# Low parts one piece behind the high parts in the paired products, and transposes two turns later

## The chip, the cores and the metric

The kernel runs on one core of one Trainium2 chip. A core has TensorE (PE, matrix products into PSUM; its weight loads are listed as PEld), VectorE (DVE), ScalarE (ACT), GpSimd (POOL) and SyncE (SP), which issues the transfers. Each engine works through its own queue of instructions in order, and waits for others by semaphores. The metric is the device time of one execution in microseconds, the median of the runs.

## The reference, cut to what matters

The reference is a two-block network on 256 tokens of width 2048, all in float32. The change touches only the last part of the second block, its feed-forward layer (`D_FF` is 5632):

```python
h2 = _rmsnorm(x, ffn_norm_w[l])
g, u = jnp.split(jnp.einsum('bsd,df->bsf', h2, w_gate_up[l]), 2, axis=-1)
x = x + jnp.einsum('bsf,fd->bsd', jax.nn.silu(g) * u, w_down[l])
return _rmsnorm(x, final_norm_w)
```

## The kernel before

All products are made in near-float32 accuracy from a number format with fewer bits. Each operand is split into a high part (ScalarE copies it into the shorter format) and a low part (VectorE subtracts the high part from the original). A product is then three matmuls: high by high, low by high, high by low. The activations are split once. The weights stream from HBM in pieces of 256 x 512 numbers (512 KB), and each piece is split as it arrives: `hl` (line 382) puts ScalarE's copy (line 385, tile `wh`) and VectorE's subtraction (line 386, tile `wl`) into the queues one behind the other.

A plain product (`Job`, `Chunk`) has 512 columns of weights; a chunk is one piece, and its twelve matmuls (lines 139 to 142) are two tiles of 128 tokens, two slices of 128 rows, three matmuls each.

The feed-forward layer has eleven blocks of 512 columns, j = 0 to 10, each with a gate and an up product. Block 0 is made of plain products. Blocks 1 to 10 are paired products (`Pair`): the first half of the inner dimension is worked as four quads, in which the four half-products of gate and up are had from seven instead of eight (P1 to P7) with sums of weights in place of one of them; the second half is plain chunks. A quad has four parts (`QuadPart`):

- g: a raw gate piece, for P1 and P2 (6 matmuls, lines 255 to 257);
- u: half of a raw up piece, for P3 (3 matmuls);
- t: two sums of raw pieces made on VectorE (`formt`, line 318), the second independent of the first, for P5 and P7 (6 matmuls);
- v: two more sums (`formv`), the second reading the first, for P6 and P4 (6 matmuls).

The list of pieces of a pair is g, u, t, v, and a gate chunk c (`PairChunk`, lines 201 to 204), four times over, and then four up chunks. At the end of the fourth quad ScalarE copies P1, P5, P7 and P6 out of PSUM (tile `ps`), and GpSimd adds them up in four operations. After the fourth gate chunk `ga_evac` makes the gate (two VectorE sums into `sg`, two SiLUs on ScalarE). After the last up chunk `ub_evac` finishes the block on VectorE (tiles `up` and `sg`).

The block is then transposed for the down product. `finish` in `ffn` (line 1830) adds a small routine, `later`, that goes on by turns: at a turn TensorE transposes half of the block (four transposes into PSUM, line 363, tile `sp`), at the next turn ScalarE and VectorE split the result (tiles `ah` and `al`), and the same again for the other half. A turn comes after each u, v and chunk (`p.side`), not after g or t.

The order of everything is written out by `drive` (line 494): before the matmuls of piece i are put into TensorE's queue, `feed` has put the splits of the pieces up to i + 4 into ScalarE's and VectorE's queues, and their loads into SyncE's. What an evacuation or a turn of `later` adds comes behind those. `la` is the distance, 3 at first and 4 from block 1 on, when `wide` (line 1894) is called. At most `nraw` raw pieces (5 from then on) are loaded and not yet dropped.

All large tiles come from 43 buffers (`Slots`), given out in the order in which they were given back. Who gets a buffer waits for the last reader of its old content. A raw piece is given back when its low part is queued, g and u when v has been formed; high and low parts when the piece's matmuls are queued; t and v in the split of v.

After blocks 0 to 3, 4 to 7 and 8 to 10 there are down products (`fd`) over what is ready: four column blocks of eight chunks in the first two thirds, five in the last. In the first of the four, a chunk waits by `needs` until the block that it reads has been transposed: block 3, 7 or 10 is needed at the seventh, seventh and fifth chunk; if its `later` has turns left then, they are taken at once (`force`).

Of the kernel before, what the change touches and what calls it, by code (L numbers as in the profile page):

```python
# [9 lines left out]
F32 = mybir.dt.float32  # L10
F32R = mybir.dt.float32r
# [5 lines left out]
P = 128  # L17
# [10 lines left out]
RAW = 4  # L28
LA = 3
# [85 lines left out]
class Chunk(Piece):  # L115
# [4 lines left out]
        self.job, self.ks, self.n = job, ks, job.n  # L120
        self.w = job.w[ks[0] * P:(ks[-1] + 1) * P, job.n0:job.n0 + job.n].rearrange("(k p) n -> p k n", p=P)

    def split(self, b):
        self.wh, self.wl = b.hl(self.raw, len(self.ks), self.n)
        b.drop(self.raw)

    def prod(self, b, outs=None, tiles=range(2)):
# [90 lines left out]
class QuadPart(Piece):  # L218
# [2 lines left out]
    def __init__(self, pair, q, raws, names, first, last):  # L221
        self.pair, self.q, self.raws, self.names, self.first, self.last = pair, q, raws, names, first, last

    def split(self, b):
        g, u = self.raws.get("g"), self.raws.get("u")
        if self.w is not None:
            self.raws[self.kind] = self.raw
        if self.kind == "g":
            self.wh, self.wl = b.hl(self.raw, 2, 512)
        elif self.kind == "u":  # L230
            self.wh, self.wl = b.hl(self.raw[:, 1:2], 1, 512)
        elif self.kind == "t":
            t = self.raws["t"] = b.slots.get([P, 2, 512], F32, "formt")
            b.tt(t[:, 0], u[:, 0], g[:, 0], ALU.subtract, b.teng[0])
            b.tt(t[:, 1], u[:, 1], u[:, 0], ALU.subtract, b.teng[1])
            self.wh, self.wl = b.hl(t, 2, 512)
        else:
            t, v = self.raws["t"], b.slots.get([P, 2, 512], F32, "formv")
            b.tt(v[:, 0], u[:, 1], t[:, 0], ALU.subtract, b.teng[2])
            b.tt(v[:, 1], g[:, 1], v[:, 0], ALU.subtract, b.teng[3])  # L240
            self.wh, self.wl = b.hl(v, 2, 512)
            b.drop(g)
            b.drop(u)
            b.slots.put(t, v)

    def prod(self, b):
        P_, q = self.pair.p, self.q
# [42 lines left out]
class Builder:  # L290
# [88 lines left out]
        for t in ts:  # L379
            self.abanks.append(self.bof.pop(id(t))[1])  # L380

    def hl(self, src, nk, n):

        wh, wl = self.slots.get([P, nk, n], F32R, "wh"), self.slots.get([P, nk, n], F32R, "wl")
        self.nc.scalar.activation(wh, src, AF.Copy)  # L385
        self.nc.vector.tensor_tensor(wl, src, wh.bitcast(F32), op=ALU.subtract)  # L386
        return wh, wl

    def drop(self, raw):
        self.slots.put(raw)  # L390
# [82 lines left out]
    def split_first(self, k):  # L473

        p = self.all[0]
        if k == 0:
            p.wh, p.wl = self.slots.get([P, KG, 512], F32R, "wh"), self.slots.get([P, KG, 512], F32R, "wl")
        self.act(p.wh[:, k], p.raw[:, k])
        self.tt(p.wl[:, k], p.raw[:, k], p.wh[:, k].bitcast(F32), ALU.subtract)
        if k == KG - 1:  # L480
            self.drop(p.raw)
            self.ns = 1

    def feed(self, n):

        while True:
            while self.nd < len(self.loads) and self.live < self.nraw:
                self.load()
            if self.ns >= min(n, len(self.all)):
                break  # L490
            self.all[self.ns].split(self)
            self.ns += 1

    def drive(self):
        self.all = [p for j in self.jobs for p in j.pieces()]
        self.loads = [p for p in self.all if p.w is not None]
        self.nd = self.ns = self.live = 0
        self.nraw, self.la = RAW, LA
        self.feed(0)
        self.begin()  # L500
        for i, p in enumerate(self.all):
            if p.begin:
                p.begin()
            self.feed(i + 1 + min(self.la, 1 + i // RAMP))
            if type(p) is Chunk and p.job.evac is None:
                break
            for ev in p.needs:
                self.force(ev)
            p.prod(self)
            p.done(self)  # L510
            if p.side:
                self.side()

        for t in range(2):
            for c, p in enumerate(self.all[i:]):
                o = self.acc()
                p.prod(self, {t: o}, [t])
                self.last_evac(t, c, o)
                self.free(o)
            self.finish(t)  # L520
# [1289 lines left out]
    def ffn(self):  # L1810
# [19 lines left out]
        def finish(j, s):  # L1830
            h, l = sl.get([P, 4, 256], F32R, f"ah{j}"), sl.get([P, 4, 256], F32R, f"al{j}")
            aT[j] = (h, l)

            def later():
                for b in range(2):
                    yield 1
                    p = self.ps()
                    for jj in range(2):
                        for t in range(2):
                            self.tr(p[:, jj * 256 + t * P:jj * 256 + (t + 1) * P], s[:, t, (2 * b + jj) * P:(2 * b + jj + 1) * P])  # L1840
                    yield 1
                    fl = lambda a: a[:, 2 * b:2 * b + 2, :].rearrange("p a b -> p (a b)")
                    self.split(fl(h), fl(l), p)
                sl.put(s)
                self.done(f"aT{j}")
            self.add(later(), urgent=True)
            if j == 10:
                for v in h3 + list(self.sx.values()):
                    sl.put(*v)
# [44 lines left out]
        def wide():  # L1894

            self.abanks = deque(list(range(4, 7)) + list(self.abanks))
            self.sbanks = deque([7])
            self.nraw, self.la = 5, 4

        ak = lambda k: (aT[k // 4][0][:, k % 4, :], aT[k // 4][1][:, k % 4, :])  # L1900
        xs = lambda q, i: [v[:, i, q % 2, :] for v in self.sx[q // 2]]
# [91 lines left out]
```

## Time and profile before

| what | value |
|---|---|
| median of 3 runs | 2350.32 us (2348.36 to 2350.64) |
| profiled execution, its own time | 2351.64 us |
| its span, first to last instruction | 2349.4 us |
| mean granted TensorE clock | 0.984 |
| busy: TensorE / VectorE / ScalarE / GpSimd | 96% / 66% / 49% / 17% |
| HBM over the span | 175 GB/s |
| ten paired products (three stretches together) | 530.5 us |
| first two down products | 89.0 and 89.5 us |

Rows of the profile give, for a group, its line, engine and operation, the tile written and those read, the number of instructions, and their time; in views by time the first number is the start in microseconds and the second the stretch that the merged instructions take, with the idle time before it and what ended it in brackets. A granted clock below 1 means that TensorE ran slower, as it does behind a pause. Matmuls overlap in the pipeline, so that a row of 0.39 us comes every 0.23 us, and a TensorE that is shown as busy may still have lost time.

### The profile page before, as it was taken

The page shows a single profiled execution, that of the slowest core. Times are in us where ns is not written, and L with a number is a line of the kernel's source. Part 1 is how long each engine was busy: PE and PEld are TensorE (multiplying, and loading weights), DVE is VectorE, ACT ScalarE, POOL GpSimd, SP SyncE. Part 2 cuts the span into 40 slices and gives each one's busy share as a digit, 9 for nine tenths or more (in the row PEclk, how much of TensorE's full clock was granted, in tenths as well). Part 3 has the DMA queues.
Part 4 walks back from the last instruction along what each step waited for, and adds up shares of the span by engine and source line. Part 5 has one row for each costly group of instructions (what it writes and reads, how often), then busy time and mean ns, then how long its engine had stood idle before and what let it go on. Part 6 is the DMA issues. An engine that isn't in the chain of part 4 may idle for free.

```text
span 2349.4 us, 27772 instructions
## 1 busy us (share of the span) xinstructions
PE 2254.9 (96%) x10396; PEld 1863.1 (79%) x10396; DVE 1541.1 (66%) x1774; ACT 1145.1 (49%) x1532; POOL 399.2 (17%) x284
## 2 busy tenths in 40 slices
PE   9999999999999999999999999998899888998898
PEld 7888888888888888888888888876678666786676
DVE  5775776456566554556867865657765777747774
ACT  6634545546545443445555544534453444534453
POOL 2020104004232010002733521101110111101111
PEclk9999999999999999999999999999999999999899
DMA  9655555464565566665455565645465444655472
GB/s 313 189 176 185 157 174 172 152 199 151 161 197 179 181 185 202 202 199 183 147 163 161 161 187 183 198 141 161 144 205 181 145 153 150 206 161 180 144 247 75
DMA packets 215046, 413.99 MB, mean 176 GB/s; under 512 B 13538, under 2 KB 20432, under 8 KB 214912
## 3 DMA queue, kind: packets, MB, share of 16 engines
q1 hardware_dynamic: 211968, 405.99, 54.5%
q0 software_dynamic: 2224, 5.13, 0.7%
q8 instruction: 81, 1.33, 0.2%
q10 hardware_dynamic: 720, 1.11, 0.1%
q14 instruction: 53, 0.43, 0.1%
HBM read 408.51 MB, written 3.67 MB: 175 GB/s over the span
## 4 chain that ended last, share of the span: by engine, by line
PE 66%; DVE 10%; ACT 5%; issue 4%; POOL 1%; ACTq 0%; DVEq 0%; POOLq 0%
PE acc L139 19%; PE acc L140 19%; PE acc L142 19%; DVE wl L386 5%; ACT wh L385 4%; PE sp L343 3%; DVE formv L318 2%; PE sp L363 2%; DVE formt L318 2%; POOL ps L318 1%; PE acc L201 1%; PE acc L202 1%; ACT ps L314 1%; PE acc L204 1%; DVE up L318 0%
## 5 line engine op out<-in xcount | busy, mean ns | idle before, releaser
L386 DVE TENSOR_TENSOR wl<-raw,wh 128x1024 fp32r<-128x1024 f32 (+2 forms) x763 | 956.5, 1292 | 318.2 <-ACT wh L385 274.6
L385 ACT ACTIVATE wh<-raw 128x1024 fp32r<-128x1024 f32 (+2 forms) x763 | 743.7, 1025 | 154.7 <-DVE wl L386 93.1
L139 PE MATMUL acc<-wh,xh 128*128 128x512 f32 (+2 forms) x864 | 339.8, 393 | 0.0
L140 PE MATMUL acc<-wh,xl 128*128 128x512 f32 (+2 forms) x864 | 336.2, 389 | 0.0
L142 PE MATMUL acc<-wl,xh 128*128 128x512 f32 (+2 forms) x864 | 230.5, 389 | 0.0
L139 PE MATMUL acc<-wh,h2h 128*128 128x512 f32 x512 | 202.2, 395 | 0.0
L140 PE MATMUL acc<-wh,h2l 128*128 128x512 f32 x512 | 199.4, 389 | 0.0
L142 PEld LDWEIGHTS acc<-wl,xh 128*128 128x128 f32 x864 | 162.8, 188 | 32.9
L140 PEld LDWEIGHTS acc<-wh,xl 128*128 128x128 f32 x864 | 162.7, 188 | 31.0
L139 PEld LDWEIGHTS acc<-wh,xh 128*128 128x128 f32 x864 | 162.7, 188 | 30.7
L318 POOL TENSOR_TENSOR ps<-ps 128x512 f32<-128x512 f32 x40 | 66.0, 1649 | 670.9 <-ACT ps L314 668.6
L139 PE MATMUL acc<-wh,ah 128*128 128x512 f32 x352 | 137.5, 391 | 0.0
L140 PE MATMUL acc<-wh,al 128*128 128x512 f32 x352 | 137.0, 389 | 0.0
L142 PE MATMUL acc<-wl,h2h 128*128 128x512 f32 x512 | 136.9, 389 | 0.0
L201 PE MATMUL acc<-wh,h3h 128*128 128x512 f32 x320 | 127.2, 397 | 0.0
L202 PE MATMUL acc<-wh,h3l 128*128 128x512 f32 x320 | 126.7, 396 | 0.0
L142 PEld LDWEIGHTS acc<-wl,h2h 128*128 128x128 f32 x512 | 96.1, 188 | 20.0
L385 ACT ACTIVATE wh<-formt 128x1024 fp32r<-128x1024 f32 x40 | 42.4, 1060 | 141.8 <-DVE formt L318 141.8
L140 PEld LDWEIGHTS acc<-wh,h2l 128*128 128x128 f32 x512 | 96.2, 188 | 18.9
L139 PEld LDWEIGHTS acc<-wh,h2h 128*128 128x128 f32 x512 | 96.2, 188 | 19.0
L385 ACT ACTIVATE wh<-formv 128x1024 fp32r<-128x1024 f32 x40 | 42.3, 1058 | 118.2 <-DVE formv L318 112.2
L142 PE MATMUL acc<-wl,ah 128*128 128x512 f32 x352 | 94.8, 389 | 0.0
(492 smaller groups left out, 3844.2 us busy)
## 6 DMA issues: line engine op xcount, KB each, us to landing
raw<-in_w_in_dram SPq DMA_DIRECT2D x328, 512.0 KB, 3.7
raw<-in_w_gate_up_dram SPq DMA_DIRECT2D x176, 512.0 KB, 4.1
raw<-in_w_down_dram SPq DMA_DIRECT2D x88, 512.0 KB, 4.0
raw<-in_w_out_dram SPq DMA_DIRECT2D x64, 512.0 KB, 3.8
raw<-in_w_branch_dram SPq DMA_DIRECT2D x48, 512.0 KB, 3.9
raw<-in_w_mem_kv_dram SPq DMA_DIRECT2D x31, 512.0 KB, 6.8
raw<-in_w_in_dram SPq DMA_DIRECT2D x8, 464.0 KB, 3.4
raw<-in_w_in_dram SPq DMA_DIRECT2D x8, 448.0 KB, 3.4
```

Source lines behind the costliest of these rows:

```text
L139: b.nc.tensor.matmul(outs[t], x, self.wh[:, kk], start=self.first and kk == 0, stop=False)
L140: b.nc.tensor.matmul(outs[t], y, self.wh[:, kk], start=False, stop=False)
L142: b.nc.tensor.matmul(outs[t], x, self.wl[:, kk], start=False, stop=self.last and kk == len(self.ks) - 1)
L201: b.nc.tensor.matmul(outs[t], x, self.wh[:, kk], start=self.first and kk == 0 and t == 1, stop=False)
L202: b.nc.tensor.matmul(outs[t], y, self.wh[:, kk], start=False, stop=False)
L204: b.nc.tensor.matmul(outs[t], x, self.wl[:, kk], start=False, stop=self.last and kk == len(self.ks) - 1)
L314: self.nc.scalar.activation(out, in_, func, **k)
L318: (self.nc.vector if eng == "v" else self.nc.gpsimd).tensor_tensor(out, a, b, op=op)
L343: self.nc.tensor.matmul(out, lhsT, rhs, start=start, stop=stop)
L363: self.nc.tensor.transpose(out, in_, self.ident if k == P else self.ident[:k, :k])
L385: self.nc.scalar.activation(wh, src, AF.Copy)
L386: self.nc.vector.tensor_tensor(wl, src, wh.bitcast(F32), op=ALU.subtract)
```

## The change

In the paired products and all that follows them, a piece's split is taken apart. `hi` puts the sums (for t and v) and ScalarE's high part into the queues; `lo` puts VectorE's low part there. `feed` lets `hi` run `ahead` pieces in front of `lo`: 0 until `wide`, 1 from then on. So the low part of a piece follows the sums and the high part of the next piece. The pieces whose low parts are queued before the matmuls of piece i are the same as before. g's and u's raw pieces are given back in `hi` of v, which now stands ahead of t's low part; t and v are given back each with its own low part.

In `later` the first half's transposes wait three turns instead of one; the second half's follow as before, so that all of it is two turns later. A down product's first turns are affected too: for block 10 two turns remain when the fifth chunk needs it.

```diff
@@ class Chunk
-    def split(self, b):
-        self.wh, self.wl = b.hl(self.raw, len(self.ks), self.n)
+    def hi(self, b):
+        self.src = self.raw
+        self.wh = b.hi(self.src)
+
+    def lo(self, b):
+        self.wl = b.lo(self.src, self.wh)
         b.drop(self.raw)
@@ class QuadPart
-    def split(self, b):
+    def hi(self, b):
         g, u = self.raws.get("g"), self.raws.get("u")
         if self.w is not None:
             self.raws[self.kind] = self.raw
         if self.kind == "g":
-            self.wh, self.wl = b.hl(self.raw, 2, 512)
+            self.src = self.raw
         elif self.kind == "u":
-            self.wh, self.wl = b.hl(self.raw[:, 1:2], 1, 512)
+            self.src = self.raw[:, 1:2]
         elif self.kind == "t":
-            t = self.raws["t"] = b.slots.get([P, 2, 512], F32, "formt")
+            t = self.src = self.raws["t"] = b.slots.get([P, 2, 512], F32, "formt")
             b.tt(t[:, 0], u[:, 0], g[:, 0], ALU.subtract, b.teng[0])
             b.tt(t[:, 1], u[:, 1], u[:, 0], ALU.subtract, b.teng[1])
-            self.wh, self.wl = b.hl(t, 2, 512)
         else:
             t, v = self.raws["t"], b.slots.get([P, 2, 512], F32, "formv")
+            self.src = v
             b.tt(v[:, 0], u[:, 1], t[:, 0], ALU.subtract, b.teng[2])
             b.tt(v[:, 1], g[:, 1], v[:, 0], ALU.subtract, b.teng[3])
-            self.wh, self.wl = b.hl(v, 2, 512)
             b.drop(g)
             b.drop(u)
-            b.slots.put(t, v)
+        self.wh = b.hi(self.src)
+
+    def lo(self, b):
+        self.wl = b.lo(self.src, self.wh)
+        if self.kind in "tv":
+            b.slots.put(self.src)
@@ class Builder
-    def hl(self, src, nk, n):
-
-        wh, wl = self.slots.get([P, nk, n], F32R, "wh"), self.slots.get([P, nk, n], F32R, "wl")
+    def hi(self, src):
+
+        wh = self.slots.get(src.shape, F32R, "wh")
         self.nc.scalar.activation(wh, src, AF.Copy)
+        return wh
+
+    def lo(self, src, wh):
+        wl = self.slots.get(src.shape, F32R, "wl")
         self.nc.vector.tensor_tensor(wl, src, wh.bitcast(F32), op=ALU.subtract)
-        return wh, wl
+        return wl
...
     def feed(self, n):
 
+        n = min(n, len(self.all))
         while True:
             while self.nd < len(self.loads) and self.live < self.nraw:
                 self.load()
-            if self.ns >= min(n, len(self.all)):
+            if self.ns >= n:
                 break
-            self.all[self.ns].split(self)
+            while self.nh < min(self.ns + 1 + self.ahead, len(self.all)):
+                self.all[self.nh].hi(self)
+                self.nh += 1
+            self.all[self.ns].lo(self)
             self.ns += 1
...
@@ ffn, finish, later
                 for b in range(2):
-                    yield 1
+                    yield 1 if b else 3
                     p = self.ps()
...
@@ ffn, wide
-            self.nraw, self.la = 5, 4
+            self.nraw, self.la, self.ahead = 5, 4, 1
```

More of the change, by code (lines that the diff above doesn't have):

```diff
@@ L481, in split_first @@
             self.drop(p.raw)
-            self.ns = 1
+            self.ns = self.nh = 1
     def feed(self, n):
+        n = min(n, len(self.all))
         while True:
@@ L496, in drive @@
         self.loads = [p for p in self.all if p.w is not None]
-        self.nd = self.ns = self.live = 0
-        self.nraw, self.la = RAW, LA
+        self.nd = self.nh = self.ns = self.live = 0
+        self.nraw, self.la, self.ahead = RAW, LA, 0
         self.feed(0)
```

## The prediction

> **What bounds the kernel now.** I read the stages of the run first (busy time of each engine in chosen stretches), then the waits inside one of them, then VectorE's and TensorE's instructions in order of time. The change touches only the feed-forward part, which begins near 1500 us. The first three rows below are the ten paired products (1 to 3, 4 to 7, 8 to 10), the last two the down products between them. (A pair ends 10.1 us after GpSimd's sums in it begin, 1614.28 - 1604.14 in rows below; I laid the bounds by that.)
>
> ```profile
> core 0: us, PE busy (x) PEld busy (x) DVE busy (x) ACT busy (x) POOL busy (x), PEclk, DMA share, GB/s
> 1562.50:1724.24 161.74, 137.24 (x565) 106.47 (x564) 124.86 (x141) 80.88 (x98) 19.78 (x12) 0.94 0.49 160
> 1813.20:2025.07 211.87, 181.06 (x740) 140.61 (x739) 163.36 (x184) 103.37 (x125) 26.39 (x16) 0.94 0.50 166
> 2114.60:2271.46 156.86, 136.81 (x552) 106.41 (x551) 121.01 (x136) 77.08 (x93) 20.87 (x14) 0.93 0.53 174
> 1724.24:1813.20 88.96, 87.99 (x392) 72.62 (x392) 49.40 (x50) 35.33 (x36) 0.00 (x0) 1.00 0.55 173
> 2025.07:2114.60 89.53, 89.53 (x400) 73.91 (x399) 49.47 (x50) 35.43 (x36) 0.00 (x0) 1.00 0.54 171
> ```
>
> In the down products TensorE is busy 99 to 100% of the time at full clock: nothing on VectorE can speed them up. In the paired products, 530.5 us together, no engine is busy all the time and the granted clock is 0.94. The rhythm shows in GpSimd's four sums, once per pair:
>
> ```profile
> 1604.14 6.83 POOL L318 TENSOR_TENSOR ps<-ps 128x512 f32<-128x512 f32 x4 [72.85 <-ACT ps L314]
> 1659.08 6.83 POOL L318 TENSOR_TENSOR ps<-ps 128x512 f32<-128x512 f32 x4 [48.12 <-ACT ps L314]
> 1714.10 6.83 POOL L318 TENSOR_TENSOR ps<-ps 128x512 f32<-128x512 f32 x4 [48.19 <-ACT ps L314]
> ```
>
> A pair takes 55.0 us (1714.10 - 1659.08). VectorE's instructions show why; this is the last quad of a pair, the rest of that pair, and the start of the next:
>
> ```profile
> 1589.28 2.96 DVE L386 TENSOR_TENSOR wl<-raw,wh 128x1024 fp32r<-128x1024 f32 x3
> 1592.15 1.28 DVE L318 TENSOR_TENSOR formt<-raw 128x512 f32<-128x512 f32 x2
> 1594.62 1.23 DVE L386 TENSOR_TENSOR wl<-formt,wh 128x1024 fp32r<-128x1024 f32 x1 [1.19 <-ACT wh L385]
> 1595.77 0.68 DVE L318 TENSOR_TENSOR formv<-raw,formt 128x512 f32<-128x512 f32 x1
> 1596.48 0.69 DVE L318 TENSOR_TENSOR formv<-raw,formv 128x512 f32<-128x512 f32 x1
> 1598.36 1.23 DVE L386 TENSOR_TENSOR wl<-formv,wh 128x1024 fp32r<-128x1024 f32 x1 [1.18 <-ACT wh L385]
> 1599.50 3.60 DVE L386 TENSOR_TENSOR wl<-raw,wh 128x1024 fp32r<-128x1024 f32 x3
> 1603.60 1.23 DVE L386 TENSOR_TENSOR wl<-raw,wh 128x1024 fp32r<-128x1024 f32 x1 [0.50 <-ACT wh L385]
> 1605.04 2.02 DVE L386 TENSOR_TENSOR wl<-raw,wh 128x1024 fp32r<-128x1024 f32 x1 [0.21 <-ACT wh L385]
> 1606.99 0.68 DVE L318 TENSOR_TENSOR sg<-acc,ps 128x512 f32<-128x512 f32 x1
> 1608.25 0.69 DVE L318 TENSOR_TENSOR sg<-acc,ps 128x512 f32<-128x512 f32 x1 [0.58 <-POOL ps L318]
> 1610.68 1.97 DVE L386 TENSOR_TENSOR wl<-raw,wh 128x1024 fp32r<-128x1024 f32 x2 [1.74 <-ACT wh L385]
> ...
> 1619.92 0.68 DVE L318 TENSOR_TENSOR up<-acc,ps 128x512 f32<-128x512 f32 x1
> ...
> 1622.69 2.96 DVE L386 TENSOR_TENSOR wl<-raw,wh 128x1024 fp32r<-128x1024 f32 x3
> ```
>
> VectorE is never waiting for TensorE here. It forms a sum, waits 1.19 us until ScalarE has rounded it, subtracts, forms the next sum, waits 1.18 us again. From 1589.28 to 1599.50 one quad takes it 10.22 us: low parts of c, g and u 2.87; sum t until its low part starts 2.47; that low part 1.15; sum v until its low part 2.59; that low part 1.14. A 1024-wide low part thus has a pitch of 1.14 and a 512-wide one 0.59. TensorE follows behind:
>
> ```profile
> 1598.38 0.50 PE L255 MATMUL acc<-wh,sh 128*128 128x512 f32 x1 [1.28 <-ACT wh L385]
> ...
> 1600.67 0.40 PE L201 MATMUL acc<-wh,h3h 128*128 128x512 f32 x1
> ...
> 1603.40 0.39 PE L201 MATMUL acc<-wh,h3h 128*128 128x512 f32 x1
> ...
> 1614.28 0.39 PE L255 MATMUL acc<-wh,h3h 128*128 128x512 f32 x1
> ```
>
> ```profile
> 1621.54 0.45 PE L363 MATMUL sp<-ident,sg 128*128 128x128 f32 x1 [5.05 <-DVE sg L327]
> ...
> 1630.04 0.60 PE L363 MATMUL sp<-ident,sg 128*128 128x128 f32 x4
> 1630.39 0.48 PE L255 MATMUL acc<-wh,h3h 128*128 128x512 f32 x1
> ```
>
> The twelve matmuls of a chunk take 2.73 us (1600.67 to 1603.40), 0.2275 each. So the 33 of a quad with its chunk need 7.5 us, and a pair (180, and two groups of four transposes at 0.35) 41.65. TensorE could run a pair in 41.65, VectorE is busy 41 us per pair ((124.86 + 163.36 + 121.01) / 10), and the difference is waiting: for ScalarE in every quad, and once per pair TensorE's transposes, which stand behind the next pair's first two pieces and wait 5.05 us for sg.
>
> **The change part by part.** *Low parts one piece later.* VectorE's order in a quad becomes: low c, low g, both sums of t, low u, both sums of v, low t, low v. Nothing is added to any engine. Two independent 512-wide operations follow at 0.60:
>
> ```profile
> 1629.18 0.68 DVE L318 TENSOR_TENSOR al<-sp,ah 128x512 fp32r<-128x512 f32 x1
> 1629.78 0.68 DVE L318 TENSOR_TENSOR formv<-raw,formt 128x512 f32<-128x512 f32 x1
> ```
>
> So t's sums occupy 1.20, v's dependent sums 0.71 + 0.60 = 1.31 (1596.48 - 1595.77, then a pitch). t's high part is ready 2.47 after its sums start; u's low part (0.60) and v's sums fill 3.11, no wait is left. v's is ready 2.59 after its sums start, and 1.31 + 1.14 = 2.45 are filled: 0.14 of waiting. The quad: 2.28 + 1.20 + 0.60 + 1.31 + 1.14 + 0.14 + 1.14 = 7.81 instead of 10.22. Saved 2.41, four times a pair: 9.64. What hides ScalarE's rounding now is u's low part and v's sums; without that cover each of the two costs its 1.2 again.
>
> The other waits of that VectorE view also go, because the high part is already queued on ScalarE before the copies of P1, P5, P7, P6 and the two SiLUs: 0.50, 0.21, 1.74, and 0.58 since sg comes no earlier relative to GpSimd's sums. That is 3.03.
>
> *What is late next: GpSimd beside VectorE.* The low part at 1605.04 took 2.02 instead of 1.23 while the sums ran. With its waits gone, VectorE issues low parts without a gap through the 6.83 us of the four sums. What continuous work beside GpSimd costs shows earlier in this trace, where two low parts (2.37 alone) took 4.52:
>
> ```profile
> 1277.94 4.52 DVE L386 TENSOR_TENSOR wl<-raw,wh 128x1024 fp32r<-128x1024 f32 x2
> ```
>
> ```profile
> 1276.89 2.50 POOL L318 TENSOR_TENSOR nkb<-nkb,nfb 128x512 f32<-128x512 f32 x1
> 1279.47 1.90 POOL L318 TENSOR_TENSOR nfb<-nfb 128x512 f32<-128x512 f32 x1
> ```
>
> That is 1.07 a piece; the row in the pair says 0.79. Bounds for a pair: from the 0.79 paid already up to four times 1.07 = 4.3. The fourth sum meets sg, which has one operand in PSUM and kept its 0.68 beside the sums, so I take three at 0.87 = 2.6, near the row of the pair itself: 1.8 more than now.
>
> The Trainium skill, SBUF — State Buffer, section "Who interferes with whom", says that a VectorE instruction with two SBUF inputs and a GpSimd instruction that reads SBUF exclude each other for a whole instruction, by order of issue. By that rule each of the three sums holds up one low part, which speaks against this change and would give the 2.6; were the one stretched row all there is, a pair would come out 1.8 shorter. The trace agrees with the rule in the 2.02 and the 4.52.
>
> *Transposes two turns later.* They move behind the next pair's first chunk, that is behind t (6 matmuls), v (6) and c (12). sg is done by VectorE 2.77 us after the pair's end (1619.92 to 1622.69), TensorE arrives after 33 matmuls, 7.5 us: the 5.05 us stall and the slow matmuls behind it go. Behind the transposes stand g1 and the rest on TensorE, and ScalarE's ah and VectorE's al, two turns later; the second ah now stands behind the high parts of v2 and c2 on ScalarE, which I price at 0.35 on VectorE. sg's buffer is held two turns longer. At a down product's entry the transposes wait about 1 us today and won't:
>
> ```profile
> PEld sp L363 <- DVE sg L327: 1.2, 1, 1.2
> ```
>
> In the last third two of the turns are forced before the fifth chunk, between 0 and 1.6 (a copy to ah, taken as long as the 0.68 of al, and al itself, with their signals, if the chunk waits for them); I take 0.5.
>
> *Buffers and loads.* A high part held one piece longer takes one more of 43 buffers, so a load or a high part may wait for a later product. Loads land well ahead now:
>
> ```profile
> DMA to landing us min/median/max: 3.5/4.0/6.5
> ```
>
> Five pieces are in flight, each held for landing (4.0), the wait until its sums or low part, and that work: by the pitches above 9.3 for g (4.0 and 5.3 until v's sums have read it), 8.3 for u, 6.3 for c, 24 us of the 5 x 7.8 = 39 that the buffers offer in a quad. The rate rises from 160 to about 200 GB/s; the page's 40 slices reach that elsewhere:
>
> ```profile
> GB/s 313 189 176 185 157 174 172 152 199 151 161 197 179 181 185 202 202 199 183 147 163 161 161 187 183 198 141 161 144 205 181 145 153 150 206 161 180 144 247 75
> ```
>
> Taken at nothing; bounds 0 and one landing exposed per quad.
>
> *The sum.* Steady pair: 55.0 - 9.64 - 3.03 + 1.8 + 0.35 = 44.5; added up from the pitches (4 x 7.81, four low parts 4.56, sg 1.25, up and sg 2.77, al 1.2 + 0.35, sums 2.6) it is 44.0. I take 44.1. That is above TensorE's 41.65, so VectorE still sets the pace and TensorE waits some 2.5 us, mostly at the low part of the fourth t. The first pair after a down product has no transposes and no old up to finish, and VectorE starts full: 41; the second inherits part of that: 43.2; pair 1, behind a plain product, 43. Together 43 + 44.1 x 2, 41 + 43.2 + 44.1 x 2, 41 + 43.2 + 44.1 = 432, against 530.5: 98.6 less. Entries of the down products: 3 x 1 - 0.5 = 2.5 less. The profiled execution has
>
> ```profile
> span 2349.4 us, 27772 instructions
> ```
>
> and 2351.64 us in all, so 2251 after; the median of the runs lies 1.3 below the profiled one: **2250 us**, 4.3% less.
>
> **The rivals.** *TensorE becomes the bound.* If GpSimd's sums cost VectorE no more than the one 0.79, VectorE's pair is 42.2, and the same walk through TensorE's order gives 42.3 to 42.6 with one short wait at the fourth t. Seven pairs then gain 1.6 more: 2239. For it: VectorE is busy just 124.86 us in three pairs. Against: the 4.52.
>
> *Half the waits stay.* The high part of v can stand on ScalarE behind a copy that waits for TensorE, or its buffer behind a product (near the end of a third few of the 43 are free). Then one 1.19 per quad stays: 40 x 1.19 = 48, 2298. Against it: the waits for ScalarE's high part are the same in quads with and without copies.
>
> *Slower: loads become exposed.* One buffer fewer and high parts needed a piece earlier; if SyncE's queue issues each quad's g and u only when the products before have finished, TensorE, ScalarE and VectorE all wait for a landing. It decides from 2.5 us per quad (40 x 2.5 eats the 100); with a full 4.0 us exposed it is 160 lost against 100, 2410. For it: SyncE waits for TensorE's products today, 24.5 us in one pair:
>
> ```profile
> SPq L469 <- PE acc L257: 24.5, 7, 9.1
> ```
>
> Against it: the 24 of 39 us.
>
> *Nothing happens.* VectorE's 1.19 could return as waits for TensorE's evacuations, 2350; but TensorE has 13 us per pair to give.
>
> **How the numbers follow.** Forecast 0.60, TensorE bound 0.15, half the waits 0.17, slower 0.05, nothing 0.03. Around the forecast, the price of GpSimd's sums (0.8 to 4.3) moves eight pairs by -1.8 to +1.7 each: 2236 to 2264. The range for 8 in 10 takes in the TensorE-bound case and reaches towards the half-gain case: 2235 to 2280. A difference under 0.2% (4.7 us) can't be told from no change here. Faster 0.92, within 0.03, slower 0.05.
>
> **What would show it.** GpSimd's sums 44 us apart instead of 55.0; VectorE waiting for formt's and formv's high part for under 0.3 us instead of 1.19; the transposes without a wait; two or three low parts per pair of about 2.0 us near the sums; TensorE's waits gathered at the low part of the last t. If the spacing is 42.5 and VectorE waits for TensorE at up, the first rival is right. If the waits for formv's high part stay, the second. If ScalarE's high parts wait for loads, the third. The down products must stay at 89 us; if they move, the order also matters where I took it to be hidden.

## The result and the profile after

The changed kernel takes 2259.71 us (median of 4 runs, 2258.43 to 2260.1), against 2349.76 us before beside it: a ratio of 0.9616, 95% interval 0.9600 to 0.9633. It is 90 us faster, 3.8%; 2250 had been predicted, within 2235 to 2280. The profiled execution took 2260.1 us, its span is 2258.3 us.

First the stages, as in the prediction's first view; the columns are stretch, length, busy time (and instructions) of PE, PEld, DVE, ACT, POOL, the granted clock, DMA share, GB/s. Three rows of paired products, then the first two down products:

```profile
1562.90:1698.94 136.04, 128.25 (x565) 102.85 (x564) 125.99 (x141) 81.60 (x99) 19.74 (x12) 1.00 0.55 190
1786.70:1963.40 176.70, 169.44 (x748) 137.26 (x747) 164.99 (x184) 104.01 (x126) 26.33 (x16) 1.00 0.58 195
2050.80:2181.90 131.10, 126.16 (x559) 102.68 (x558) 122.10 (x136) 77.16 (x94) 20.88 (x14) 1.00 0.57 195
1698.94:1786.70 87.76, 87.76 (x392) 72.67 (x391) 48.82 (x49) 35.30 (x36) 0.00 (x0) 1.00 0.57 183
1963.40:2050.80 87.40, 87.40 (x391) 72.34 (x391) 48.44 (x49) 34.97 (x36) 0.00 (x0) 1.00 0.56 184
```

VectorE's busy time in the first paired stretch is nearly the same as before (125.99 against 124.86), in 136 us instead of 162. No instruction was taken off any engine; waiting was. TensorE's clock in the paired products is 1.00 instead of 0.94. Before, it was 0.50 from 1621.5 to 1625.5, right behind the pause of 5.05 us, and 1.00 from 1600 to 1616; now the longest wait in a steady pair is 2.0 us, and no part of it shows a lower clock.

These bounds lie within 0.4 us of TensorE's first matmul of each stretch. Those of the kernel before do not all: its second and third paired stretch really end 1.6 us later, at 2026.72 and 2273.08, since their last pairs end 11.8 us after GpSimd's sums begin and not 10.1. With every bound at TensorE's first matmul (and the span's end behind the last), the ten pairs took 533.2 us and now take 443.0; the three down products took 89.2, 88.2 and 76.3 us and now take 88.0, 88.0 and 76.4. So the pairs gave 90 us, the down products 1.3.

GpSimd's sums, the mark of a pair, in order of time:

```profile
1598.49 6.82 POOL L326 TENSOR_TENSOR ps<-ps 128x512 f32<-128x512 f32 x4 [66.80 <-ACT ps L322]
1644.01 6.82 POOL L326 TENSOR_TENSOR ps<-ps 128x512 f32<-128x512 f32 x4 [38.71 <-ACT ps L322]
1689.54 6.82 POOL L326 TENSOR_TENSOR ps<-ps 128x512 f32<-128x512 f32 x4 [38.71 <-ACT ps L322]
```

They are 45.5 us apart; it was 55.0, and 44.1 had been predicted. VectorE in order of time shows what the pair is made of: the last quad, the end of the pair and the start of the next (start, stretch, operation, idle time before it and what ended that):

```profile
1630.61 2.35 DVE L398 TENSOR_TENSOR wl<-raw,wh 128x1024 fp32r<-128x1024 f32 x2
1632.88 1.29 DVE L326 TENSOR_TENSOR formt<-raw 128x512 f32<-128x512 f32 x2
1634.09 0.68 DVE L398 TENSOR_TENSOR wl<-raw,wh 128x512 fp32r<-128x512 f32 x1
1634.69 0.68 DVE L326 TENSOR_TENSOR formv<-raw,formt 128x512 f32<-128x512 f32 x1
1635.41 0.69 DVE L326 TENSOR_TENSOR formv<-raw,formv 128x512 f32<-128x512 f32 x1
1636.02 1.22 DVE L398 TENSOR_TENSOR wl<-formt,wh 128x1024 fp32r<-128x1024 f32 x1
1637.29 1.23 DVE L398 TENSOR_TENSOR wl<-formv,wh 128x1024 fp32r<-128x1024 f32 x1
1638.43 4.62 DVE L398 TENSOR_TENSOR wl<-raw,wh 128x1024 fp32r<-128x1024 f32 x4
1643.48 1.23 DVE L398 TENSOR_TENSOR wl<-raw,wh 128x1024 fp32r<-128x1024 f32 x1 [0.42 <-ACT wh L393]
1644.62 0.68 DVE L326 TENSOR_TENSOR sg<-acc,ps 128x512 f32<-128x512 f32 x1
1647.26 0.69 DVE L326 TENSOR_TENSOR sg<-acc,ps 128x512 f32<-128x512 f32 x1 [1.95 <-POOL ps L326]
1647.87 1.82 DVE L398 TENSOR_TENSOR wl<-raw,wh 128x1024 fp32r<-128x1024 f32 x1
1649.61 2.38 DVE L326 TENSOR_TENSOR formt<-raw 128x512 f32<-128x512 f32 x2
```

The quad from 1630.61 to 1638.43 takes 7.82 us, with no wait for ScalarE listed (from t's low part to v's it takes 1.27 instead of a pitch of 1.14, so 0.13 is left). The other waits stand at the pair's end. The second sg waits 1.95 us for GpSimd. Behind it a low part takes 1.82 instead of 1.22 and the sums of t 2.38 instead of 1.28, while GpSimd's last two sums run: 1.70 us. VectorE never waits for TensorE in this stretch, so it still sets the pace.

Why GpSimd is late is on ScalarE, in order of time, from the high part of v to the copy of P6. The first two rows are the kernel before, the others the changed one:

```profile
1597.27 1.06 ACT L385 ACTIVATE wh<-formv 128x1024 fp32r<-128x1024 f32 x1 [2.68 <-DVE formv L318]
...
1603.45 0.60 ACT L314 ACTIVATE ps<-acc 128x512 f32<-128x512 f32 x1
```

```profile
1636.20 1.06 ACT L393 ACTIVATE wh<-formv 128x1024 fp32r<-128x1024 f32 x1 [0.87 <-DVE formv L326]
1637.16 1.99 ACT L393 ACTIVATE wh<-raw 128x1024 fp32r<-128x1024 f32 x2
1639.06 0.57 ACT L322 ACTIVATE ps<-acc 128x512 f32<-128x512 f32 x1
1639.54 2.00 ACT L393 ACTIVATE wh<-raw 128x1024 fp32r<-128x1024 f32 x2
1641.43 1.07 ACT L322 ACTIVATE ps<-acc 128x512 f32<-128x512 f32 x2
1642.38 1.06 ACT L393 ACTIVATE wh<-raw 128x1024 fp32r<-128x1024 f32 x1
1643.33 0.60 ACT L322 ACTIVATE ps<-acc 128x512 f32<-128x512 f32 x1
```

There is no idle time behind v's high part. Five high parts of chunks, one more than before, and the copies of P1, P5 and P7 stand in front of the copy of P6, which starts at 1643.33; TensorE's last matmul for P6 had started at 1638.90. From v's high part to that copy it is 7.13 us; it was 6.18. GpSimd's first two sums, on which the second sg depends, can only start behind it, while VectorE comes to sg sooner than before. (That the copy would come in time further ahead in ScalarE's queue was not tried.)

TensorE's weight loads (the first sign of its waits) around the start of the next pair, only the rows with over 0.5 us of idle time:

```profile
1612.84 0.19 PEld L263 LDWEIGHTS acc<-wh,h3h 128*128 128x128 f32 x1 [0.80 <-DVE up L326]
...
1620.17 0.19 PEld L265 LDWEIGHTS acc<-wl,sh 128*128 128x128 f32 x1 [1.06 <-DVE wl L398]
...
1624.31 0.42 PEld L371 LDWEIGHTS sp<-ident,sg 128*128 128x128 f32 x4 [2.01 <-DVE al L326]
```

The 5.05 us in front of the first transposes are gone. There is a new wait of 2.0 us in front of the second group: from block 1 on all transposes go through one PSUM bank, and the second group may overwrite it only when al has been made from the first.

### The profile page after: what moved, and what is told of

Same layout as the page of the kernel before. It is cut to its first block, busy times and chain, and to the rows that moved or that the text cites. A ratio compares the mean times of both kernels' runs of the same rounds, so it can differ in the third digit from the quotient of the medians.

```text
span 2258.3 us, 27824 instructions
## 1 busy us (share of the span) xinstructions
PE 2219.7 (98%) x10396; PEld 1849.6 (82%) x10396; DVE 1542.7 (68%) x1774; ACT 1145.4 (51%) x1532; POOL 399.1 (18%) x284
## 3 DMA queue, kind: packets, MB, share of 16 engines
q8 instruction: 81, 1.33, 0.2%
## 4 chain that ended last, share of the span: by engine, by line
PE 76%; DVE 5%; ACT 2%; issue 2%; POOL 1%; ACTq 0%; DVEq 0%; POOLq 0%
PE acc L143 20%; PE acc L144 20%; PE acc L146 20%; PE sp L351 3%; DVE wl L398 2%; PE sp L371 2%; PE acc L205 2%; PE acc L206 2%; PE acc L208 2%; PE acc L263 2%; PE acc L264 2%; PE acc L265 2%; ACT wh L393 1%; DVE formt L326 1%; DVE formv L326 1%
## 5 line engine op out<-in xcount | busy, mean ns | idle before, releaser
L208 PE MATMUL acc<-wl,h3h 128*128 128x512 f32 x320 | 85.6, 389 | 0.0
```

The costliest lines, as they stand in the source:

```text
L208: b.nc.tensor.matmul(outs[t], x, self.wl[:, kk], start=False, stop=self.last and kk == len(self.ks) - 1)
```

## The experiments

**The order of the low parts alone.**

```diff
-                    yield 1 if b else 3
+                    yield 1
```

> The new order of low parts alone; the transposes again wait one turn. Theory (VectorE paces the changed kernel, TensorE has about 4 us to spare in a pair): the transposes stand behind u again and wait for sg, which VectorE finishes 2.8 us (its lateness at a pair's end now) + 2.77 after the pair's end; TensorE comes there after 2.0, so it stalls 3.5 us, and its matmuls behind that are slow for some 1.4 us. That uses up what it has to spare: pairs of 46.5 to 48 instead of 45.5, in all 2268 to 2282 us. Rival (the stall is hidden, the order is the whole gain): 2260 us. Other rival (the two parts give their gains independently, the transposes 5 us a pair): 2300 us or more.

Measured: 2267.46 us, ratio 0.9653 (0.9637 to 0.9669). GpSimd's sums (in order of time) are 46.1 and 45.7 us apart, and TensorE waits in front of both groups of transposes:

```profile
1598.80 6.81 POOL L326 TENSOR_TENSOR ps<-ps 128x512 f32<-128x512 f32 x4 [67.97 <-ACT ps L322]
1644.86 6.82 POOL L326 TENSOR_TENSOR ps<-ps 128x512 f32<-128x512 f32 x4 [39.24 <-ACT ps L322]
1690.58 6.84 POOL L326 TENSOR_TENSOR ps<-ps 128x512 f32<-128x512 f32 x4 [38.91 <-ACT ps L322]
```

```profile
1658.67 0.14 PEld L371 LDWEIGHTS sp<-ident,sg 128*128 128x128 f32 x1 [1.00 <-PE acc L265]
1660.00 0.31 PEld L371 LDWEIGHTS sp<-ident,sg 128*128 128x128 f32 x3 [1.19 <-DVE sg L335]
1667.77 0.42 PEld L371 LDWEIGHTS sp<-ident,sg 128*128 128x128 f32 x4 [2.15 <-DVE al L326]
```

So the order alone gives 82 of the 90 us. I had expected a longer stall, which would have set the pace, and a time from 2268 us up. The stall is 2.2 us before the first group, not 3.5: I had taken over the changed kernel's lateness of VectorE at a pair's end, 2.8 us, and here it is 1.2 (the pair ends at 1655.90 on TensorE, and `up` starts at 1657.09). The pairs stay with VectorE, and a spacing of the sums is longer than in the changed kernel by 0.5 us at the most. The transposes' place gives 7.8 us here. Of that 1.7 us lie in the seven spacings, and 5.0 us at the ends of the three paired stretches: there TensorE finishes the last pair 11.0 us after GpSimd's sums begin, instead of 9.4.

**The later transposes alone.**

```diff
-            self.nraw, self.la, self.ahead = 5, 4, 1
+            self.nraw, self.la, self.ahead = 5, 4, 0
```

> The later transposes alone; the high parts don't run ahead. Theory (VectorE's chain of 55.0 us a pair never waits for TensorE): GpSimd's sums stay 55.0 us apart, only the about 1 us at each of three entries into a down product and the first pair's start go, 2344 to 2349 us. Rival (TensorE's 5.05 us stall per pair was on the path): 7 pairs x 5 us less, about 2312 us.

Measured: 2347.63 us (10 runs), ratio 0.9993 (0.9983 to 1.0002). Sums in order of time:

```profile
1603.87 6.82 POOL L326 TENSOR_TENSOR ps<-ps 128x512 f32<-128x512 f32 x4 [72.73 <-ACT ps L322]
1658.87 6.82 POOL L326 TENSOR_TENSOR ps<-ps 128x512 f32<-128x512 f32 x4 [48.17 <-ACT ps L322]
```

The pairs are 55.0 us apart, as before. TensorE's 5.05 us stall was real and cost nothing, since VectorE's chain did not wait for TensorE anywhere in the pair. The waiting only moved: at the start of the next pair TensorE now stands 2.9 us for a high part, and the granted clock of the paired products is still 0.94. The two parts don't add up: the second is worth under 4 us alone (1.6 between the medians) and about 8 behind the first.

**No sums on GpSimd.**

```diff
-                b.tt(p6, p6, p1, ALU.add, "g")
-                b.tt(p7, p7, p6, ALU.add, "g")
-                b.tt(p6, p6, p5, ALU.add, "g")
-                b.tt(p5, p5, p7, ALU.add, "g")
```

> The changed kernel without GpSimd's four sums (the gate and up products lack their combination: the copies P1, P6, P7, P5 are used as they are). Theory (VectorE paces; a pair of 45.5 holds 1.95 of waiting for GpSimd's second sum and 1.7 by which operations beside the sums are stretched): 3.65 us less VectorE time, until TensorE's 41.65 and its waits bound the pair at 42 to 43; nine pairs x 2.5 to 3.5, 2228 to 2238 us. Rival (TensorE's waits at a pair's start, for up and for the one bank that the transposes use, pace it): pairs stay at 45.5, 2256 to 2260 us.

Measured: 2241.4 us, ratio 0.9542 (0.9528 to 0.9556). VectorE in order of time, first the end of one pair, then of the next:

```profile
1640.15 1.28 DVE L322 TENSOR_TENSOR sg<-acc,ps 128x512 f32<-128x512 f32 x2
1641.35 1.22 DVE L394 TENSOR_TENSOR wl<-raw,wh 128x1024 fp32r<-128x1024 f32 x1
1642.48 1.29 DVE L322 TENSOR_TENSOR formt<-raw 128x512 f32<-128x512 f32 x2
...
1648.90 0.69 DVE L322 TENSOR_TENSOR up<-acc,ps 128x512 f32<-128x512 f32 x1 [0.80 <-PE acc L208]
...
1682.82 1.28 DVE L322 TENSOR_TENSOR sg<-acc,ps 128x512 f32<-128x512 f32 x2
```

The wait before the second sg and both stretched operations are gone. A pair takes 42.7 us (1682.82 - 1640.15), TensorE is busy for 41.98 of it, and now VectorE waits for TensorE at up: TensorE has become the bound. This is the prediction's first rival, made by hand, near the time that it was given (42.3 to 42.6 a pair, 2239 us). So GpSimd's sums cost the changed kernel 18 us, and TensorE's waits at a pair's start don't set its pace. The total is 3 us above the range that I expected: seven spacings of the pairs gave 17.5 us, and those across a down product gave nothing.

**The sums in another order**, one of them as soon as P7 is copied:

```diff
+            if self.kind == "t":
+                b.tt(P_["P7s"], P_["P7s"], P_["P1s"], ALU.add, "g")
...
-                b.tt(p6, p6, p1, ALU.add, "g")
                 b.tt(p7, p7, p6, ALU.add, "g")
+                b.tt(p6, p6, p1, ALU.add, "g")
```

> The changed kernel with the sums in another order: P7 + P1 as soon as P7 is copied, so that one sum instead of two stands between the copy of P6 and the second sg; five sums instead of four. Theory: sg's wait of 1.95 falls by one sum, to 0.3 to 0.6; the added sum stretches at most one low part by 0.8; net 0.6 to 1.5 us a pair, 2246 to 2254 us. Rival (TensorE's waits pace it): 2258 to 2260 us.

Measured: 2261.25 us, ratio 0.9626 (0.9612 to 0.9641): no better than the changed kernel's 0.9616. VectorE in order of time at the same place:

```profile
1642.04 1.81 DVE L400 TENSOR_TENSOR wl<-raw,wh 128x1024 fp32r<-128x1024 f32 x1 [0.42 <-ACT wh L395]
1643.77 0.68 DVE L328 TENSOR_TENSOR sg<-acc,ps 128x512 f32<-128x512 f32 x1
1645.03 0.69 DVE L328 TENSOR_TENSOR sg<-acc,ps 128x512 f32<-128x512 f32 x1 [0.58 <-POOL ps L328]
1645.63 1.81 DVE L400 TENSOR_TENSOR wl<-raw,wh 128x1024 fp32r<-128x1024 f32 x1
1647.37 3.47 DVE L328 TENSOR_TENSOR formt<-raw 128x512 f32<-128x512 f32 x2
```

The wait for GpSimd fell from 1.95 to 0.58, as expected. But the stretching rose from 1.7 to 0.6 + 0.6 + 2.2 = 3.4: VectorE waits in front of sg or, sooner or later, inside its own operations. 0.58 + 3.4 = 4.0 against 3.65. The pairs are 45.8 us apart, 0.3 more, as that says. My expectation of a gain was wrong because it counted one more stretched operation, and there were two. The total lies near the rival's, but not for its reason: VectorE waits for TensorE nowhere in the pair. An earlier sum at the price of a fifth gains nothing; the order alone, with four sums, was not tried.

**The four sums on VectorE, from PSUM** (ScalarE copies P1 alone):

```diff
-                b.tt(p6, p6, p1, ALU.add, "g")
-                b.tt(p7, p7, p6, ALU.add, "g")
-                b.tt(p6, p6, p5, ALU.add, "g")
-                b.tt(p5, p5, p7, ALU.add, "g")
+                b.tt(p6, P_["P6"], p1, ALU.add)
+                b.tt(p7, P_["P7"], p6, ALU.add)
+                b.tt(p6, P_["P5"], p6, ALU.add)
+                b.tt(p5, P_["P5"], p7, ALU.add)
```

> The changed kernel with all four sums on VectorE, read straight from the PSUM banks of P6, P7 and P5 (ScalarE copies P1 alone). Theory (GpSimd's sums cost VectorE 1.95 of waiting and 1.7 of stretched operations a pair, 3.65 in all, because the two don't run two-SBUF-operand work side by side): instead come four operations with one PSUM operand at a pitch of 0.6 to 0.7, 2.4 to 2.8; pairs of 44.2 to 44.7 instead of 45.5, 2246 to 2253 us. Rival (VectorE has no waiting to give back there; the four operations come on top): 47.9 a pair, 2278 us or more.

Measured: 2247.59 us, ratio 0.9564 (0.9550 to 0.9578). VectorE in order of time:

```profile
1640.85 2.73 DVE L327 TENSOR_TENSOR ps<-acc,ps 128x512 f32<-128x512 f32 x4
1643.50 1.22 DVE L399 TENSOR_TENSOR wl<-raw,wh 128x1024 fp32r<-128x1024 f32 x1
```

Four operations more on the engine that sets the pace make the kernel 12 us faster than the changed one: they occupy 2.65 us, and 3.65 us of waiting and stretching go, with the 0.42 us that ScalarE's now shorter queue no longer causes. The pairs are 43.9 us apart. The rival, that they come on top, is out.

**Two sums on VectorE, two on GpSimd** (ScalarE copies P1 and P5 alone).

```diff
-                b.tt(p6, p6, p1, ALU.add, "g")
-                b.tt(p7, p7, p6, ALU.add, "g")
+                b.tt(p6, P_["P6"], p1, ALU.add)
+                b.tt(p7, P_["P7"], p6, ALU.add)
                 b.tt(p6, p6, p5, ALU.add, "g")
                 b.tt(p5, p5, p7, ALU.add, "g")
```

> The first two sums (the ones that sg waits for) on VectorE from PSUM, the last two on GpSimd. Theory: the 1.95 of waiting goes for 1.2 to 1.4 of work; the two GpSimd sums still stretch up to two operations by 0.6 to 1.1 each, 1.2 to 2.2; pairs of 44.3 to 45.3, 2247 to 2257 us, not better than all four on VectorE. Rival (only the wait costs, the stretching falls where VectorE has time): pairs of 43.8 to 44.0, 2242 to 2245 us, better than all four on VectorE.

Measured: 2245.49 us, ratio 0.9557 (0.9542 to 0.9573), the fastest of the kernels that compute everything; its interval overlaps that of the one before, so the 2 us between the two medians are not settled. VectorE in order of time:

```profile
1638.92 1.41 DVE L328 TENSOR_TENSOR ps<-acc,ps 128x512 f32<-128x512 f32 x2
1640.25 1.22 DVE L400 TENSOR_TENSOR wl<-raw,wh 128x1024 fp32r<-128x1024 f32 x1
1641.38 1.28 DVE L328 TENSOR_TENSOR sg<-acc,ps 128x512 f32<-128x512 f32 x2
1642.58 1.22 DVE L400 TENSOR_TENSOR wl<-raw,wh 128x1024 fp32r<-128x1024 f32 x1
1643.71 2.38 DVE L328 TENSOR_TENSOR formt<-raw 128x512 f32<-128x512 f32 x2
```

Two sums on VectorE occupy 1.33 us; the two on GpSimd stretch only formt, by 1.1. It came out between the two expectations in time, and at the rival's in spacing: 43.7 us a pair. The stretching costs, against the rival, but only one of the two sums stretched anything. By the rows' times the first (1640.48 to 1642.62) ran beside a low part that had begun before it and then beside sg, which reads one operand from PSUM; that this is the reason was not tried by itself.

## Why the prediction was right, and where it was off

The direction, the range and the likeliest case held: VectorE set the pace, and its waits for ScalarE were what the change removed. Point by point:

- *The quad.* Predicted 7.81 us, measured 7.82. The experiment with the order alone shows that this is where the gain is.
- *The other waits (3.03 taken off).* Here the sum failed. The 1.74 is gone. Of 0.50 + 0.21, 0.42 stayed. And the 0.58, which was to go "since sg comes no earlier relative to GpSimd's sums", became 1.95. The step looked at the time of the products on TensorE and passed over ScalarE's queue, in which the copy of P6 now stands behind one more high part. VectorE got faster at the pair's end, and the copy came 0.95 us later behind v's high part.
- *GpSimd beside VectorE.* Predicted 2.6 of stretching, measured 1.70 (0.60 and 1.10); while VectorE stands in front of sg, the first two sums meet nothing. Waiting and stretching together are 3.65. That this lies within the bounds of 0.79 to 4.3 is partly luck, for they had been drawn for stretching alone.
- *The pair.* 44.1 + 1.95 + 0.42 - 0.9 = 45.57; measured 45.52. That mis-sized pair is most of the miss. Pairs 2, 3, 6, 7 and 10 took 45.5 to 45.8: 7 us over the figures used. Pairs 5 and 9 took 44.3 instead of 43.2: 2 us. Pair 1 took 45.0 instead of 43: 2 us. The pairs right behind a down product took 40.8, with 41 predicted. Together 443.0 instead of 432; against the 533.2 of the kernel before that is 90.2 saved, with 98.6 predicted.
- *Transposes.* The stall of 5.05 went, as said, but the second group got a wait of 2.0 for al, through the one bank, which the prediction did not see. "The transposes without a wait" was wrong by half. Neither sets the pace: the stall had cost nothing before (0.9993 for the turns alone), so its removal was not a gain to count in the pairs, and it had not been counted there. TensorE does wait about as much as said, 2.6 us in a pair of 45.5, but in the pair's first 17 us and not at the fourth t's low part.
- *Entries of the down products.* Predicted 2.5 us less, measured 1.3. The wait of about 1 us, read at the first entry, was taken for all three; at the second and third it was 0.3 on the weight loads, and those down products gained 0.2 and nothing. The two forced turns of the third, priced at 0.5, show next to no cost (76.3 us before, 76.4 now).
- *Buffers and loads.* Taken at nothing, and the waits of the paired stretch name no load. The rate rose to 190 to 195 GB/s.
- *The rivals.* TensorE as the bound is not what happened, but with the sums taken away it is, at 2241.4 us. Half the waits staying, loads exposed and no change at all are out by the quad's 7.82.

## What to carry to other kernels

Where two engines hand each piece to and fro, queue the first engine's step one piece ahead, and count what is then queued in front of every other operation of that engine: one more piece of early work delayed here the copy on which the next engine waited. An operation moved to an idle engine is not free if that engine and the busy one hold each other up; four sums cost VectorE 3.65 us from GpSimd and 2.65 us when it did them itself. A stall on an engine that does not set the pace was worth nothing here until the pace changed: 1.6 us alone, 7.8 behind the first part.

## What the runs showed of the hardware

Two things I had not expected. Waiting and stretching changed places almost one for one: with one sum earlier and five instead of four, VectorE waited 1.37 us less and its operations became 1.7 us longer. And which operation is stretched depends on what VectorE does at that moment: the last two sums cost it 1.7 us in the changed kernel and 1.1 us where the first of them fell mostly beside sg. The Trainium skill, SBUF — State Buffer, section "Who interferes with whom", says that a VectorE instruction with at most one SBUF input, outside the modes that use both of its ports, does not contend with GpSimd; the unstretched sg rows (0.68 and 0.69 beside the sums) agree.
